# A 4-byte constant that takes 64 bytes, and a last tile finished by halves of columns, in a fused hybrid decoder layer

## The chip, the cores and the metric

The kernel runs on one core of a Trainium2 chip. The metric is the device time of one execution in microseconds; the median of three runs stands for a kernel. One further execution is taken by the hardware profiler, and all rows shown below come from it.

## The reference

The kernel computes one layer of a decoder trunk in float32, for one sequence of 512 positions and a width of 1024. Cut to what matters here:

```python
h = rmsnorm(x, norm_mix_g)
proj = h @ w_in                                  # 1024 x 9232
bg, cg, xv, q, k, v, z, a, b, ga, gb = split(proj)
y_a = (bg * causal_dwconv(cg * xv, conv_a_w)) @ w_a_out
y_b = gated_delta_net(q, k, v, z, a, b) @ w_b_out     # 8 heads, chunked scan
x = x + (sigmoid(ga) * y_a + sigmoid(gb) * y_b) @ w_o
h = rmsnorm(x, norm_ffn_g)
up = causal_dwconv(h @ w_up, ffn_conv_w)         # 1024 x 5632
gate, val = split(up)
x = x + (silu(gate) * val) @ w_down              # 2816 x 1024
out = rmsnorm(x, norm_final_g)
```

## The kernel before, in words

**Products.** Each float32 factor is split into a rounded part and a rest, both of type float32r (`wh` and `wl` for weights, pairs such as `hT0/hT1`, `xs0/xs1` for activations). A product is three TensorE matmuls: rest by rounded, rounded by rest, rounded by rounded. All of them go through one helper, `mm`, so in the profile they share line L108 and are told apart by their tiles' names. In the name "ps<-hT,wh" the two operands stand in the order of the alphabet. A matmul has a stationary operand of 128 by 128, loaded by a weight load of its own (PEld), and a moving operand of 512 or 256 columns.

**Stages, in order.** The input products with `hT` (q, k, v, z, gates; the delta-net scan runs between them), the sum jobs on `ts` and `hT` (Winograd-like forms with moving tiles of 256 columns, `sum_job`), the product with `w_a_out` on `yas`, with `w_b_out` on `yb`, with `w_o` on `mix` and `mixb`, the products with `w_up` on `h` (tiles `h20`, `h21`) and sum jobs on `us`, and last the product with `w_down` on `xs`. In the products with `hT`, `h`, `ts`, `us`, `yas` and `yb` the weights are stationary and the activations move; in those with `mix`, `mixb` and `xs` the activations are stationary and the weights move, 512 columns at a time.

**Where tiles lie.** Tiles come from pools that are stacked from the low end of each partition's memory, or from the high end where a pool says `side="right"`. Each buffer is rounded up to 32 bytes. The pool `const` lies lowest; its first tile is `gate`, 4 bytes on one partition, which takes 32 bytes (1152 to 1184). After it come `ident`, `nhalf`, `phalf`, `wA` and `wF`, and then the pool `wp` with `raw`, `wh` and `wl`, from byte 2816, which is 0 modulo 64. All large tiles of the low stack (`raw`, `wh`, `wl`, `hT`, `yb`, `h2`, `x1`, `kqs` and the delta-net's tiles) start at 0 modulo 64; the tiles of x in the first stage stand at 32. The high stack ends at byte 229344, which is 32 modulo 64, and its large tiles (`ts`, `us`, `xs`, `yas`, `ya`, `mixa`, `mix`, `mixb`, `aTa`, `aTb`) all start at 32 modulo 64. Slices that a matmul takes of a tile start at multiples of 512 bytes within it.

**The order of work.** DMAs, ScalarE (ACT), VectorE (DVE) and GpSimd (POOL) instructions are placed by a list scheduler that follows the order of the program and data dependences; within `tc.manual_schedule` the named engines keep the written order. `gate` is written by `feed`, a one-element GpSimd copy that makes the GpSimd queue wait for a weight block before it issues further DMAs.

**The end.** The product with `w_down` runs in jobs: `use_a` (first pass), `use_c`, `use_b` for all pairs of rows but the last `LAST` = 4, then `use_t(0)`, `use_t(1)` and `use_l` for these four. There are four tiles of 128 positions, t = 0 to 3, with 1024 columns in two halves of 512 (`HALVES`). `use_t(1)` finishes the accumulation of tiles 0 and 1 and calls `fin2` for each; `use_l` finishes the lower half of tiles 2 and 3, which stand in the PSUM banks `v4[0]` and `v4[1]`, 12 matmuls of 512 columns each, and calls `fin2`. The upper halves of tiles 2 and 3 stand in the banks `r[0]` and `r[1]`; they were finished after `use_c` by `fin2_hi`, which leaves the partial norm in `st["r", t]` and the half, multiplied by the norm's weights but not yet by r, in `st["y", t][1]`, so those banks are free by then. For each half, `fin2` adds the bank to `x1`, squares and sums it on ACT, multiplies by the norm's weights on DVE, then forms r (DVE), raises it to -0.5 (POOL), scales one half on DVE and one on ACT, and issues two output DMAs from the SP queue.

Of the kernel before, what the change touches and what calls it, by code (L numbers as in the profile page):

```python
# [9 lines left out]
F32 = mybir.dt.float32  # L10
F32R = mybir.dt.float32r
AF = mybir.ActivationFunctionType
ALU = mybir.AluOpType
# [3 lines left out]
P = 128  # L17
S = 512
NT = S // P
D = 1024  # L20
# [5 lines left out]
EPS = 1e-6  # L26
# [34 lines left out]
def layer_kernel(ctx, tc, x, norm_mix_g, w_in, w_ab, conv_a_w, gdn_conv_w, gdn_A_log, gdn_dt_bias,  # L61
                 gdn_norm_g, w_a_out, w_b_out, w_o, norm_ffn_g, w_up, ffn_conv_w, w_down,
                 norm_final_g, out):
    nc = tc.nc
    pe, act, dve, pool = nc.tensor, nc.scalar, nc.vector, nc.gpsimd
    x2 = x[0]
    out2 = out[0]
# [3 lines left out]
    const = ctx.enter_context(tc.tile_pool(name="const", bufs=1))  # L71
# [4 lines left out]
    def nm(s):  # L76
        cnt[0] += 1
        return f"{s}{cnt[0]}"
# [8 lines left out]
    def advance(queue, n):  # L87
        while n and queue:
            queue[0].step()
            if queue[0].done:  # L90
                queue.popleft()
            else:
                n -= 1

    def tick():
        advance(backs, 1)
        advance(mids, 1)
        advance(chains, 1)
        advance(evacs, 2)
        advance(splits, 1)  # L100
        advance(sums_of, 1)
# [5 lines left out]
    def mm(o, a, b, start, stop, free=False):  # L107
        pe.matmul(o, lhsT=a, rhs=b, start=start, stop=stop, skip_group_check=free)  # L108
        nmm[0] += o.shape[-1]
        if nmm[0] >= SLAB * S:  # L110
            nmm[0] -= SLAB * S
            tick()
# [12 lines left out]
    class Block:  # L125
# [78 lines left out]
    def run_jobs(jobs):  # L204
        jobs[1][0].load()
        for i, (block, use) in enumerate(jobs):
            Task(block.split()).finish()
            drain(splits)
            if i + 1 < len(jobs):
                splits.append(Task(jobs[i + 1][0].split()))  # L210
            for j, (later, _) in enumerate(jobs[i + 2:i + 5]):
                if later.lead >= j + 2:
                    later.load()
            if adds and i + 2 < len(jobs) and jobs[i + 2][0].fed:
                feed(jobs[i + 2][0].raw)
            use(block.wh, block.wl)


    gate = const.tile([1, 1], F32, name="gate")

    def feed(raw):
        el = raw[0:1, 1].rearrange("p k n -> p (k n)") if len(raw.shape) == 4 else raw[0:1, 1]
        tc.keep_in_program_order(pool.tensor_copy(out=gate, in_=el[:, 0:1]))  # L223
        advance(adds, FEED)


# [43 lines left out]
    def sum_job(w, i, xs, sums, consume, place, pre=None):  # L270
        def use(wh, wl):
# [73 lines left out]
    nhalf = const.tile([P, 8], F32, name="nhalf")  # L345
# [11 lines left out]
    def pair_out():  # L357
        return room["pool"].tile([P, 2 * S], F32, tag="o", bufs=room.get("o", 3), name=nm("o"))
# [22 lines left out]
    HS = S // 2  # L381
# [633 lines left out]
    st = {}  # L1015
# [7 lines left out]
    LAST = 4  # L1023
# [176 lines left out]
    FORMS_A, FORMS_T, FORMS_B = (("v2", 1), ("v3", 2), ("v1", 3)), (("21", 0), ("22", 2)), (("v4", 1),)  # L1200
# [41 lines left out]

    def times_b(banks, xs, slot, names, tau, wh, wl, q=None, start=False, stop=False):
        for name, i in names:
            o, w = banks["11" if name == "21" else name][tau], name if q is None else (name, q)
            times(o, xs, slot, i, tau, wh[w], wl[w], start and name != "21", stop, name == "21")

    def open_banks(banks, names):
        for name in names:
# [47 lines left out]
    HALVES = [slice(0, S), slice(S, D)]  # L1297
# [167 lines left out]
    def prep_d(prep, c):  # L1465
        return Task(prep(ffn_pairs(down_w.pairs[2 * c], 2), xs(), 2 * c % 4))
# [28 lines left out]
    def use_b(p):  # L1495
        def use(wh, wl):
            if p % 2 == 0 and p // 2 + 1 < N7 // 2:
                splits.append(prep_d(prep_b, p // 2 + 1))
            for name in (*FORMS_T, *FORMS_B):
                for tau in range(2):  # L1500
                    times_b(d_banks, xs(), p % 4, (name,), tau, wh, wl)
            if p == N7 - LAST - 1:
                splits.append(prep_d(prep_b, N7 // 2 - 1))
        return use


    def use_t(q):
        def use(wh, wl):
            for tau in range(2):
                for i in range(2):  # L1510
                    times_b(d_banks, xs(), (N7 - LAST + 2 * q + i) % 4, FORMS_T, tau, wh, wl, i, False, q + i == 2)
                if q == 1:
                    fin2(tau, [d_banks["11"][tau], d_banks["22"][tau]])
        return use

    def use_l(wh, wl):
        for tau in range(2):
            for i in range(LAST):
                times_b(d_banks, xs(), (N7 - LAST + i) % 4, FORMS_B, tau, wh, wl, i, False, i == LAST - 1)
            fin2(tau + 2, [d_banks["v4"][tau]])  # L1520

    def fin2_hi(t):
        cvp, x1, a = st["cvp"], st["x1"], d_banks["r"][t - 2]
# [10 lines left out]
        yield  # L1534

    def fin2(t, acc):
        cvp, x1 = st["cvp"], st["x1"]
        ss = cvp.tile([P, 2], F32, tag="ss", name=nm("ss"))
        if t < 2:
            o = pair_out()  # L1540
            y, r = [o[:, sl] for sl in HALVES], cvp.tile([P, 1], F32, tag="r", name=nm("r"))
        else:
            y, r = st["y", t], st["r", t]
        for hf, a in enumerate(acc):
            sl = HALVES[hf]
            dve.tensor_tensor(out=x1[:, t, sl], in0=x1[:, t, sl], in1=a, op=ALU.add)
            act.activation(out=a, in_=x1[:, t, sl], func=AF.Square, accum_out=ss[:, hf:hf + 1])
            dve.tensor_tensor(out=y[hf], in0=x1[:, t, sl], in1=st["gfn"][:, sl], op=ALU.mult)
            if hf < len(acc) - 1:
                dve.tensor_scalar(r, ss[:, hf:hf + 1], 1.0 / D, EPS, op0=ALU.mult, op1=ALU.add)  # L1550
        dve.scalar_tensor_tensor(out=r, in0=ss[:, len(acc) - 1:len(acc)], scalar=1.0 / D, in1=r,
                                 op0=ALU.mult, op1=ALU.add)
        pool.tensor_tensor(out=r, in0=r, in1=nhalf[:, 0:1], op=ALU.pow)
        dve.tensor_scalar(y[0], y[0], r, None, op0=ALU.mult)
        act.activation(out=y[1], in_=y[1], func=AF.Copy, scale=r)
        for sl, e in zip(HALVES, y):
            nc.sync.dma_start(out=out2[t * P:(t + 1) * P, sl], in_=e)


    def down_place(i):  # L1560
# [69 lines left out]
```

## Time and profile before

| | before |
|---|---|
| median of three runs | 972.78 us (971.88 to 973.0) |
| the profiled execution's own time | 973.09 us |
| its span, first to last instruction | 971.4 us |
| granted TensorE clock, mean | 0.996 |
| PE busy | 958.7 us (99%) |
| PEld busy | 826.1 us (85%) |
| DVE, ACT, POOL busy | 744.0, 506.7, 153.4 us |
| DMA moved | 138.11 MB, mean 142 GB/s |

PE is the matmul part of TensorE, PEld its weight loads. Matmuls are pipelined: the duration of one (the third number of a group, in ns) is longer than the distance from its start to the next one's start, so the pace of a stretch is read from first and last start and the count, not from the durations. "Busy" of a group counts overlapped time once only.

### The profile page before, as it was taken

The page shows a single profiled execution, that of the slowest core. Times are in us where ns is not written, and L with a number is a line of the kernel's source. Part 1 is how long each engine was busy: PE and PEld are TensorE (multiplying, and loading weights), DVE is VectorE, ACT ScalarE, POOL GpSimd, SP SyncE. Part 2 cuts the span into 40 slices and gives each one's busy share as a digit, 9 for nine tenths or more (in the row PEclk, how much of TensorE's full clock was granted, in tenths as well). Part 3 has the DMA queues.
Part 4 walks back from the last instruction along what each step waited for, and adds up shares of the span by engine and source line. Part 5 has one row for each costly group of instructions (what it writes and reads, how often), then busy time and mean ns, then how long its engine had stood idle before and what let it go on. Part 6 is the DMA issues. An engine that isn't in the chain of part 4 may idle for free.

```text
span 971.4 us, 16140 instructions
## 1 busy us (share of the span) xinstructions
PE 958.7 (99%) x6166; PEld 826.1 (85%) x6166; DVE 744.0 (77%) x1397; ACT 506.7 (52%) x1071; POOL 153.4 (16%) x251
## 2 busy tenths in 40 slices
PE   8999999999999999999999999999999999999996
PEld 6888887887878889999988888998889998888885
DVE  5968686896725968799853479999978888968775
ACT  6796656565444434344642245555545456546463
POOL 3330300202000212312232100231222210000000
PEclk9999999999999999999999999999999999999999
DMA  6443312213121546756877435594775674075332
GB/s 225 154 138 98 116 53 88 74 58 91 52 88 49 147 121 152 184 151 158 266 222 158 119 120 207 165 244 155 164 185 177 180 154 137 37 282 204 99 130 87
DMA packets 51629, 138.11 MB, mean 142 GB/s; under 512 B 21691, under 2 KB 22112, under 8 KB 42848
## 3 DMA queue, kind: packets, MB, share of 16 engines
q1 hardware_dynamic: 39008, 107.72, 32.3%
q0 software_dynamic: 12544, 29.37, 16.1%
q8 instruction: 48, 0.79, 0.3%
q14 instruction: 29, 0.24, 0.1%
HBM read 133.64 MB, written 32.78 MB: 171 GB/s over the span
## 4 chain that ended last, share of the span: by engine, by line
PE 91%; DVE 3%; ACT 1%; issue 1%; POOL 1%; POOLq 0%
PE ps L108 83%; PE ps L681 1%; PE ps L716 1%; DVE wl L141 1%; PE ps L890 1%; PE ps L910 1%; DVE h L1326 0%; PE ps L899 0%; DVE hn L1312 0%; PE ps L878 0%; PE ps L877 0%; PE ps L854 0%; PE ps L848 0%; POOL r L1310 0%; PE ps L792 0%
## 5 line engine op out<-in xcount | busy, mean ns | idle before, releaser
L108 PE MATMUL ps<-hT,wh 128*128 128x512 f32 (+1 forms) x1104 | 319.3, 369 | 1.6 <-ACT hT L499 1.4
L140 ACT CAST wh<-raw 128x512 fp32r<-128x512 f32 x350 | 203.5, 618 | 212.6 <-PE ps L108 149.1
L141 DVE TENSOR_TENSOR wl<-raw,wh 128x512 fp32r<-128x512 f32 x350 | 233.0, 690 | 58.9 <-ACT wh L140 57.7
L108 PEld LDWEIGHTS ps<-hT,wh 128*128 128x128 f32 x1104 | 197.5, 190 | 30.6 <-ACT hT L499 1.6
L108 PE MATMUL ps<-hT,wl 128*128 128x512 f32 (+1 forms) x552 | 195.5, 362 | 0.0
L108 PE MATMUL ps<-h,wh 128*128 128x512 f32 (+1 forms) x704 | 177.8, 341 | 0.2 <-DVE h L1326 0.2
L108 PEld LDWEIGHTS ps<-h,wh 128*128 128x128 f32 x704 | 122.3, 189 | 15.4 <-DVE h L1326 0.4
L108 PEld LDWEIGHTS ps<-hT,wl 128*128 128x128 f32 x552 | 104.7, 190 | 13.8
L108 PE MATMUL ps<-h,wl 128*128 128x512 f32 (+1 forms) x352 | 114.6, 341 | 0.0
L108 PE MATMUL ps<-wh,xs 128*128 128x512 f32 x312 | 98.2, 395 | 0.0
L108 PEld LDWEIGHTS ps<-h,wl 128*128 128x128 f32 x352 | 66.6, 189 | 7.6
L108 PEld LDWEIGHTS ps<-wh,xs 128*128 128x128 f32 x312 | 58.5, 187 | 14.3
L108 PE MATMUL ps<-wl,xs 128*128 128x512 f32 x156 | 61.6, 395 | 0.0
L223 POOL COPY gate<-raw 1x1 f32<-1x1 f32 x38 | 16.9, 446 | 279.9 <-DMA raw<-in_w_in_dram 119.3
L108 PE MATMUL ps<-ts,wh 128*128 128x256 f32 x320 | 58.5, 281 | 0.0
L338 DVE SCALAR_TENSOR_TENSOR cv<-ps,wA,cv 128x511 f32<-128x511 f32 (+2 forms) x72 | 53.2, 742 | 4.0 <-ACT cv L335 3.8
L140 ACT CAST wh<-raws 128x512 fp32r<-128x512 f32 x66 | 39.2, 619 | 28.2 <-PE ps L108 16.6
L141 DVE TENSOR_TENSOR wl<-raws,wh 128x512 fp32r<-128x512 f32 x66 | 43.1, 689 | 13.4 <-ACT wh L140 13.3
L161 DVE TENSOR_TENSOR raw<-raw 128x512 f32<-128x512 f32 x72 | 49.5, 688 | 1.4
L108 PEld LDWEIGHTS ps<-ts,wh 128*128 128x128 f32 x320 | 49.8, 188 | 0.0
L108 PE MATMUL ps<-us,wh 128*128 128x256 f32 x256 | 46.8, 281 | 0.0
L108 PE MATMUL ps<-yas,wh 128*128 128x512 f32 x128 | 40.4, 395 | 0.0
(310 smaller groups left out, 1548.5 us busy)
## 6 DMA issues: line engine op xcount, KB each, us to landing
raw<-in_w_in_dram SPq DMA_DIRECT2D x35, 1024.0 KB, 4.8
raw<-in_w_up_dram SPq DMA_DIRECT2D x22, 1024.0 KB, 5.7
dv<-in_w_down_dram POOLq DMA_DIRECT2D x50, 256.0 KB, 6.0
raws<-dv SPq DMA_DIRECT2D x8, 768.0 KB, 6.8
ov<-in_w_o_dram POOLq DMA_DIRECT2D x20, 256.0 KB, 5.3
raws<-in_w_down_dram SPq DMA_DIRECT2D x10, 512.0 KB, 4.1
raw<-in_w_a_out_dram SPq DMA_DIRECT2D x4, 1024.0 KB, 5.2
raw<-in_w_b_out_dram SPq DMA_DIRECT2D x4, 1024.0 KB, 5.7
```

The lines of the kernel that those rows point to most:

```text
L108: pe.matmul(o, lhsT=a, rhs=b, start=start, stop=stop, skip_group_check=free)
L140: act.copy(out=wh, in_=src)
L141: dve.tensor_tensor(out=wl, in0=src, in1=wh.bitcast(F32), op=ALU.subtract)
L161: dve.tensor_tensor(out=r[q], in0=a, in1=b, op=op)
L223: tc.keep_in_program_order(pool.tensor_copy(out=gate, in_=el[:, 0:1]))
L338: dve.scalar_tensor_tensor(out=dst[:, sh:], in0=src[:, :S - sh], scalar=wcol(j), in1=dst[:, sh:], op0=ALU.mult, op1=ALU.add)
L681: pe.transpose(out=o[:, n * P:(n + 1) * P], in_=src[:, n * P:(n + 1) * P], identity=ident)
L716: pe.matmul(o[:, i], lhsT=kqs[:, a, h, 0, sl], rhs=kqs[:, b, h, :, sl], start=a > 0, stop=a + b == 0)
L890: pe.matmul(o[:, 0:P], lhsT=TTf[:, f, :], rhs=rs[h], start=True, stop=True)
L910: pe.matmul(o[:, 0:P], lhsT=A[:, f, :], rhs=vns[h], start=True, stop=True)
```

## The change

The tile `gate` is declared with 16 elements instead of one, so it takes 64 bytes instead of 32, and all that lies above it in the low stack moves up by 32 bytes. The high stack stays. Only one element of `gate` is written, as before.

The end is rewritten. `use_b` marks the accumulation of `v4` as stopped after its last pair. At the start of `use_t(1)` one DVE instruction adds the right 256 columns of `v4[1]` to `x1`. `use_l` finishes tile 2 as before, with 12 matmuls of 512 columns; tile 3 then runs in two parts of 256 columns, 12 matmuls each: the left one accumulates on in `v4[1]`, the right one starts afresh in the bank `r[0]`. Each part has its own add, square and step of r; the order of DVE, ACT, POOL and SP is written out by hand; half 0 of tile 2 is scaled on ACT and half 1 on DVE, half 0 of tile 3 on DVE and half 1 on ACT; the last output DMA is issued from the ACT queue. `fin2` keeps only tiles 0 and 1, with the same instructions.

```diff
-    gate = const.tile([1, 1], F32, name="gate")
+    gate = const.tile([1, 16], F32, name="gate")
...
-        tc.keep_in_program_order(pool.tensor_copy(out=gate, in_=el[:, 0:1]))
+        tc.keep_in_program_order(pool.tensor_copy(out=gate[:, 0:1], in_=el[:, 0:1]))
...
-    def times(o, xs, slot, i, tau, wh, wl, start=False, stop=False, free=False):
+    def times(o, xs, slot, i, tau, wh, wl, start=False, stop=False, free=False, cols=slice(0, S)):
         xh, xl = (e[:, slot, i, tau * P:(tau + 1) * P] for e in xs)
         for k, (a, b) in enumerate(((xl, wh), (xh, wl), (xh, wh))):
-            mm(o, a, b, start and k == 0, stop and k == 2, free)
+            mm(o[:, cols], a, b[:, cols], start and k == 0, stop and k == 2, free)
...
+    LO, HI = slice(0, HS), slice(HS, S)
+
     def use_t(q):
         def use(wh, wl):
+            if q == 1:
+                x1 = st["x1"]
+                dve.tensor_tensor(out=x1[:, 3, HI], in0=x1[:, 3, HI], in1=d_banks["v4"][1][:, HI], op=ALU.add)
...
     def use_l(wh, wl):
-        for tau in range(2):
+        x1, gfn = st["x1"], st["gfn"]
+
+        def mult(t, cols):
+            dve.tensor_tensor(out=st["y", t][0][:, cols], in0=x1[:, t, cols], in1=gfn[:, cols], op=ALU.mult)
+
+        def scale(t, hf, on_act, queue):
+            y, r = st["y", t][hf], st["r", t]
+            if on_act:
+                act.activation(out=y, in_=y, func=AF.Copy, scale=r)
+            else:
+                dve.tensor_scalar(y, y, r, None, op0=ALU.mult)
+            queue.dma_start(out=out2[t * P:(t + 1) * P, HALVES[hf]], in_=y)
+
+        def power(t):
+            pool.tensor_tensor(out=st["r", t], in0=st["r", t], in1=nhalf[:, 0:1], op=ALU.pow)
+
+        def part(t, e, a, cols, between):
+            r = st["r", t]
+            ss = st["cvp"].tile([P, 2], F32, tag="ss", name=nm("ss"))
             for i in range(LAST):
-                times_b(d_banks, xs(), (N7 - LAST + i) % 4, FORMS_B, tau, wh, wl, i, False, i == LAST - 1)
-            fin2(tau + 2, [d_banks["v4"][tau]])
+                times_b(d_banks, xs(), (N7 - LAST + i) % 4, FORMS_B, t - 2, wh, wl, i, e == 1 and i == 0, i == LAST - 1,
+                        cols, a)
+            dve.tensor_tensor(out=x1[:, t, cols], in0=x1[:, t, cols], in1=a[:, cols], op=ALU.add)
+            act.activation(out=a[:, cols], in_=x1[:, t, cols], func=AF.Square, accum_out=ss[:, e:e + 1])
+            between()
+            dve.scalar_tensor_tensor(out=r, in0=ss[:, e:e + 1], scalar=1.0 / D, in1=r, op0=ALU.mult, op1=ALU.add)
+
+        def between():
+            mult(3, LO)
+            scale(2, 0, True, nc.sync)
+
+        with tc.manual_schedule(engines={mybir.EngineType.DVE, mybir.EngineType.Activation, mybir.EngineType.Pool,
+                                         mybir.EngineType.SP}):
+            part(2, 0, d_banks["v4"][0], slice(0, S), lambda: mult(2, slice(0, S)))
+            power(2)
+            part(3, 0, d_banks["v4"][1], LO, between)
+            part(3, 1, d_banks["r"][0], HI, lambda: mult(3, HI))
+            power(3)
+            scale(2, 1, False, nc.sync)
+            scale(3, 0, False, nc.sync)
+            scale(3, 1, True, nc.scalar)
```

More of the change, by code (lines that the diff above doesn't have):

```diff
@@ L1241, in times_a, with times_b @@
                 times(banks[name][tau], xs, slot, i, tau, wh[name], wl[name], start, stop)
-    def times_b(banks, xs, slot, names, tau, wh, wl, q=None, start=False, stop=False):
+    def times_b(banks, xs, slot, names, tau, wh, wl, q=None, start=False, stop=False, cols=None, to=None):
         for name, i in names:
             o, w = banks["11" if name == "21" else name][tau], name if q is None else (name, q)
-            times(o, xs, slot, i, tau, wh[w], wl[w], start and name != "21", stop, name == "21")
+            times(o if to is None else to, xs, slot, i, tau, wh[w], wl[w], start and name != "21", stop, name == "21" or bool(cols),
+                  cols or slice(0, S))
     def open_banks(banks, names):
@@ L1500, in use @@
                 for tau in range(2):
-                    times_b(d_banks, xs(), p % 4, (name,), tau, wh, wl)
+                    times_b(d_banks, xs(), p % 4, (name,), tau, wh, wl, None, False,
+                            p == N7 - LAST - 1 and name in FORMS_B)
             if p == N7 - LAST - 1:
@@ L1536, in fin2 @@
     def fin2(t, acc):
-        cvp, x1 = st["cvp"], st["x1"]
+        cvp, x1, y = st["cvp"], st["x1"], pair_out()
         ss = cvp.tile([P, 2], F32, tag="ss", name=nm("ss"))
[L1539 to L1552, printed above, removed]
+        r = cvp.tile([P, 1], F32, tag="r", name=nm("r"))
+        for hf, sl in enumerate(HALVES):
+            dve.tensor_tensor(out=x1[:, t, sl], in0=x1[:, t, sl], in1=acc[hf], op=ALU.add)
+            act.activation(out=acc[hf], in_=x1[:, t, sl], func=AF.Square, accum_out=ss[:, hf:hf + 1])
+            dve.tensor_tensor(out=y[:, sl], in0=x1[:, t, sl], in1=st["gfn"][:, sl], op=ALU.mult)
+            if hf == 0:
+                dve.tensor_scalar(r, ss[:, 0:1], 1.0 / D, EPS, op0=ALU.mult, op1=ALU.add)
+        dve.scalar_tensor_tensor(out=r, in0=ss[:, 1:2], scalar=1.0 / D, in1=r, op0=ALU.mult, op1=ALU.add)
         pool.tensor_tensor(out=r, in0=r, in1=nhalf[:, 0:1], op=ALU.pow)
[L1554 to L1557, printed above, removed]
+        dve.tensor_scalar(y[:, HALVES[0]], y[:, HALVES[0]], r, None, op0=ALU.mult)
+        act.activation(out=y[:, HALVES[1]], in_=y[:, HALVES[1]], func=AF.Copy, scale=r)
+        for sl in HALVES:
+            nc.sync.dma_start(out=out2[t * P:(t + 1) * P, sl], in_=y[:, sl])
     def down_place(i):
```

## The prediction

> **What bounds the kernel now.** I read the profile's page first, then the chain that ended last, then the rows of single tiles.
>
> ```profile
> span 971.4 us, 16140 instructions
> PE 958.7 (99%) x6166; PEld 826.1 (85%) x6166; DVE 744.0 (77%) x1397; ACT 506.7 (52%) x1071; POOL 153.4 (16%) x251
> ...
> PE 91%; DVE 3%; ACT 1%; issue 1%; POOL 1%; POOLq 0%
> ```
>
> TensorE is busy all the time and is 91% of the chain. So the pace at which one matmul follows the next is what the time is made of. The chain in order of time shows where that holds without a break:
>
> ```profile
> 316.16 282.05 PE ps L108 x1635
> 598.24 1.41 DVE o L1260 x2
> ...
> 631.29 1.23 DVE xf L251
> ...
> 633.18 324.38 PE ps L108 x1777
> ```
>
> From 316 to 598 us and from 633 us to the end the chain is nothing but matmuls. From 598.24 to 633.18 it runs through DVE (the evacuations after the first half of `w_o`, the norm, the turns), and PE only works beside it. A faster matmul there is worth nothing.
>
> Now the pace. Two stages have the same number of matmuls, the same shape, and weights from the same buffers; only the moving tile differs. First the rows of the tile `yas`, then those of `yb` (duration min/median/max in ns, then first and last start):
>
> ```profile
> L108 PE MATMUL ps<-yas,wh x128: 395/395/397, 489.4 to 534.0; 128*128 128x512 f32 x128
> L108 PE MATMUL ps<-yas,wl x64: 396/396/397, 489.6 to 532.1; 128*128 128x512 f32 x64
> L331 ACT CAST yas<-ya x8: 608/615/622, 476.4 to 481.3; 128x512 fp32r<-128x512 f32 x8
> L332 DVE TENSOR_TENSOR yas<-ya,yas x8: 680/684/686, 478.0 to 483.1; 128x512 fp32r<-128x512 f32 x8
> ```
>
> ```profile
> L108 PE MATMUL ps<-yb,wh x128: 389/389/396, 534.2 to 577.5; 128*128 128x512 f32 x128
> L108 PE MATMUL ps<-yb,wl x64: 389/389/397, 534.4 to 575.7; 128*128 128x512 f32 x64
> ...
> L331 ACT CAST yb<-yb x8: 607/620/622, 490.1 to 493.8; 128x512 fp32r<-128x512 f32 x8
> L332 DVE TENSOR_TENSOR yb<-yb,yb x8: 682/684/693, 490.8 to 495.0; 128x512 fp32r<-128x512 f32 x8
> ```
>
> 192 matmuls make 191 steps: with `yas` 44.6 us, or 233.5 ns a step; with `yb` 43.3 us, or 226.7 ns. `yas` starts at 32 modulo 64 and the weights at 0; `yb` and the weights both start at 0. In the last stage the parts are exchanged: `xs`, at 32, is stationary and the weights, at 0, move.
>
> ```profile
> L108 PE MATMUL ps<-wh,xs x312: 388/394/397, 854.5 to 963.4; 128*128 128x512 f32 x156
> ```
>
> With the half as many of `wl` these are 468 matmuls, 467 steps in 108.9 us: 233.2 ns, the same as with `yas`. That the price is one whichever operand stands at 32 speaks for the relation of the two, not for the place of one.
>
> For moving tiles of 256 columns the sign is the other. Two adjacent windows of a sum job, first matmuls with `ts` (at 32), then with `hT` (at 0), weights at 0 in both; the columns are length, PE busy, count, clock, DMA share, GB/s:
>
> ```profile
> 379.14:384.82 5.68, 5.68 (x48) 1.00 0.96 149
> ...
> 384.82:389.12 4.30, 4.30 (x36) 1.00 0.72 242
> ```
>
> Unlike: 5.68/48 = 118.3 ns. Alike: 4.30/36 = 119.4 ns.
>
> The counts, by form (each `wh` group has half as many with `wl` beside it, since a product is three matmuls, two with `wh`):
>
> ```profile
> L108 PE MATMUL ps<-hT,wh 128*128 128x512 f32 x800 | 260.5, 400 | 0.0
> ...
> L108 PE MATMUL ps<-h,wh 128*128 128x512 f32 x384 | 119.8, 389 | 0.0
> ...
> L108 PE MATMUL ps<-h,wh 128*128 128x256 f32 x320 | 60.8, 284 | 0.2 <-DVE h L1326 0.2
> L108 PE MATMUL ps<-hT,wh 128*128 128x256 f32 x304 | 60.0, 287 | 1.6 <-ACT hT L499 1.4 <-DVE hT L503 0.3
> L108 PE MATMUL ps<-ts,wh 128*128 128x256 f32 x320 | 58.5, 281 | 0.0
> L108 PE MATMUL ps<-us,wh 128*128 128x256 f32 x256 | 46.8, 281 | 0.0
> ...
> L108 PE MATMUL ps<-wh,mix 128*128 128x512 f32 x88 | 28.2, 396 | 0.0
> ...
> L108 PE MATMUL ps<-wh,mixb 128*128 128x512 f32 x24 | 8.3, 398 | 0.0
> ```
>
> **The change, part one: 32 bytes.** It adds no instruction. Everything in the low stack goes from 0 to 32 modulo 64 and the high stack stays at 32, so every pair of weights and activations becomes alike, but at 32, and no pair of large matmul operands at 32 and 32 is in this trace. Its price is bounded by 226.7 (as two at 0) and 233.5 (as one at 32). I take 226.7, since exchanging the operands left the price at 233.2 and 233.5, which a price for the place of each operand would make a coincidence.
>
> Unlike matmuls of 512 columns: `xs` 468, `yas` 192, `mix` 132, `mixb` 36, together 828. 12 of them (tile 3) are split and counted below. From the end of `yb` at 577.7 to 598.24, 88 of the `mix` ones fit at 233 ns; the other 80 of `mix` and `mixb` lie beside the DVE chain and are counted at nothing (0.5 us more if that chain moves with them). That leaves 736. At 6.5 ns each (a little under 233.2 or 233.5 less 226.7): −4.78 us. Unlike ones of 256 columns: `ts` 480 and `us` 384, 864 at +1.1 ns: +0.95 us, all in the two unbroken stretches. Pairs that were alike (`hT`, `h`, `yb`) stay alike: nothing.
>
> ACT and DVE work on shifted tiles too. The rows L331 and L332 above are the same work on tiles at 32 (`yas`) and at 0 (`yb`): 615 against 620 and 684 against 684 ns. So nothing there, and if a few ns came, both run beside PE (DVE 77% busy). DMAs into `raw` are hidden by blocks loaded two to four jobs ahead; the page shows PE without a wait for one.
>
> **Part two: the end.** The rows of the timeline:
>
> ```profile
> 962.27 0.73 ACT L1555 ACTIVATE o<-o,r 128x512 f32<-128x512 f32 x1 [0.85 <-POOL r L1553]
> ...
> 962.90 0.58 ACT L1547 ACTIVATE ps<-x 128x512 f32<-128x512 f32 x1
> ...
> 963.45 0.39 PE L108 MATMUL ps<-wh,xs 128*128 128x512 f32 x1
> 963.64 0.16 DVE L1551 SCALAR_TENSOR_TENSOR r<-ss,r 128x1 f32<-128x1 f32 x1 [0.28 <-ACT ps L1547]
> ...
> 964.45 0.49 DVE L1554 TENSOR_SCALAR y<-y,r 128x512 f32<-128x512 f32 x1 [0.65 <-POOL r L1553]
> 964.85 0.68 DVE L1546 TENSOR_TENSOR x<-x,ps 128x512 f32<-128x512 f32 x1
> ...
> 965.62 0.60 ACT L1547 ACTIVATE ps<-x 128x512 f32<-128x512 f32 x1 [0.46 <-DVE x L1546]
> 966.16 0.19 ACT L1547 ACTIVATION_READ_ACCUMULATOR ps<-x 128x1 f32 x1
> 966.38 0.16 DVE L1551 SCALAR_TENSOR_TENSOR r<-ss,r 128x1 f32<-128x1 f32 x1
> 966.62 0.54 POOL L1553 TENSOR_TENSOR r<-r,nhalf 128x1 f32<-128x1 f32 x1 [2.21 <-DVE r L1551]
> 967.20 0.72 ACT L1555 ACTIVATE y<-y,r 128x512 f32<-128x512 f32 x1 [0.85 <-POOL r L1553]
> ```
>
> ```profile
> 967.72 0.81 SPq L1557 DMA_DIRECT2D out_dram<-y  x2
> ```
>
> The last matmul ends at 963.84, but tile 3's add starts at 964.85: DVE stood at 964.45 with tile 2's scaling, waiting for POOL. Then add, square, r, power, scale and DMA follow in a row. PE itself: 12 matmuls of 233.2 become 24 of 119.4, +0.07 us. The new add of a quarter tile in `use_t(1)` falls where DVE waits for PE and costs nothing; without that cover, 0.42 us (the 256-column row below).
>
> ```profile
> L293 DVE TENSOR_TENSOR u<-ps,u 128x256 f32<-128x256 f32 x18 | 7.6, 422 | 1.4 <-ACT u L292 1.1
> ...
> L292 ACT COPY u<-ps 128x256 f32<-128x256 f32 x18 | 6.7, 372 | 28.3 <-PE ps L108 28.3
> ```
>
> The written order puts tile 2's step of r (963.64, held by ACT, which scales tile 1 at 962.27 before it squares tile 2 at 962.90) ahead of tile 3's adds. From 963.80 on: left add 0.42, to 964.22; left square about 0.38 (estimate, from the copy's 0.37) and its read; its step of r to 964.96; right add from 964.96 to 965.38, 1.1 us after the last matmul; ACT meanwhile scales tile 2 from 964.8 to 965.5 and squares the right part to 965.9; step of r 966.07 to 966.23, power to about 966.85, scales from 966.88 (before: 967.20). ACT ends at 967.6 and issues the last DMA itself, where the second of SP's two began about 968.13. So the end comes 0.3 to 0.5 us sooner; I take −0.5. The best end is bounded by the matmuls (adds not held: −1.5), the worst by one more instruction of 0.5 us on DVE and a dearer issue from ACT, which no row shows (+0.5).
>
> **Sum.** −4.78 + 0.95 + 0.07 − 0.5 = −4.26 us. The profiled execution took 973.09 us by its own account (span 971.4), so 968.8; the median of the runs stands 0.31 below it: 968.5 us.
>
> The Trainium skill, in "TensorE: Matmul & The Clock Gate", section "Part 2: What happens when you issue a matmul", holds that the moving operand and the weights come in through two independent read ports and that loading the next weights takes nothing from the running matmul. By that rule how the two stand to each other could not matter, and part one would bring nothing, which gives 972.35 us, the same as the first rival. The trace does not agree in so far as `yas` and `yb` differ by 6.8 ns a step, but it can't exclude that the cause is another one.
>
> **Rivals.**
> 1. The pace doesn't come from the place modulo 64. All slow tiles lie in the high stack, so the cause could be which end of the memory they lie in. Then only the end changes: 973.09 + 0.07 − 0.5 − 0.31 = 972.35. For it: place and end are confounded in this trace. Against it: the operands at 32 slow 512 columns and speed 256, as a phase between two streams would, rather than a slow region. The Trainium skill's rule of two ports (the page named above) leads to the same time.
> 2. The slower one: an operand at 32 costs by itself, and two at 32 are no better than one. Then the 828 gain nothing, and the alike ones lose: `hT` 1200, `h` 576, `yb` 192, together 1968 at 6.5 ns, +12.8 us; their 936 of 256 columns gain 1.1 ns each, −1.0; with the end, 973.09 + 12.8 − 1.0 − 0.43 − 0.31 = 984.1. It decides from 229 ns on: at 2.2 ns above 226.7 the 1968 eat up the whole 4.26 us. For it: no pair at 32 has been seen. Against it: the price didn't change with the operand that stood at 32.
> 3. The pace comes as forecast, but the scheduler places tile 1's scaling ahead of the hand-written part, so that all of the end waits: +0.5 instead of −0.5, 969.5.
>
> **Chances.** Forecast 0.70, rival 3 0.05, rival 1 0.12, rival 2 0.13. The likeliest case's own range is 966.8 to 969.8: 0.5 us for the DVE stretch, up to 1 us each way for the end, 0.9 if the 256-column loss stays out. To leave out no more than 2 in 10 the range must take in rival 1: 966.8 to 972.7. A measurement of this kernel can't tell less than about 0.2% (1.95 us) from no change; forecast and rival 3 are faster by more, 0.75; rival 1 is within, 0.12; rival 2 is slower, 0.13.
>
> **What would show it.** The rows of `yas`, `xs` and `mix` at 226 to 228 ns a step and 389 ns duration; `yb`, `h`, `hT` unchanged; windows of `ts` at 119.4. `yb` at 231 or more is rival 2; `yas` at 233 is rival 1. At the end, tile 3's second add within 1.2 us of the last matmul and the last scale about 3.0 us after it (before: 3.36). The forecast is wrong first if two operands at 32 don't pace like two at 0.

## The result and the profile after

| | before | after |
|---|---|---|
| median (six runs each, same chip) | 971.87 us (970.99 to 973.0) | 965.13 us (964.45 to 967.54) |
| ratio after / before | | 0.9934, 95% interval 0.9921 to 0.9947 |
| the profiled execution's own time | 973.09 us | 966.41 us |
| its span | 971.4 us | 964.7 us |

The change makes the kernel 6.7 us faster. The forecast was 968.5 us, and its range began at 966.8: the direction came true, the size did not. Some 0.9 us of the gap between 968.5 and 965.13 are not the change's: the forecast started from 972.78 for the kernel before, which these six runs put at 971.87. One kernel below, with ten buffers for the weights, took 1920.87 and 2443.0 us in two of its six executions, at a granted clock of 1.00 in both; its 969.06 us is the median of the other four, and its paces are read from the same kernel run once more.

The page of after, its span and busy times, then the shares of its chain:

```profile
span 964.7 us, 16169 instructions
...
PE 951.5 (99%) x6178; PEld 822.6 (85%) x6178; DVE 743.1 (77%) x1401; ACT 505.9 (52%) x1073; POOL 157.1 (16%) x251
...
PE 91%; DVE 4%; ACT 1%; issue 1%; POOL 1%; POOLq 0%
```

PE does 12 matmuls more (the split of the last tile) and is busy for 7.2 us less: the matmuls follow each other faster. The chain in order of time shows where this can count:

```profile
315.98 279.38 PE ps L108 x1635
595.39 1.39 DVE o L1261 x2
...
628.55 1.23 DVE xf L251
630.43 317.85 PE ps L108 x1765
948.30 1.38 DVE x L1586 x2
```

The form is that of before: two stretches of nothing but matmuls, and the DVE stretch between them. The first matmul stretch begins where it did (315.98, before 316.16), so all but 0.2 us of the gain lies behind this point. From 948.3 us on, 9 us ahead of the last matmul's end, the chain runs through DVE, ACT and POOL.

Which stage gave it? The rows of `yas`, `yb` and `xs` (duration min/median/max in ns, first and last start in us) are three answers:

```profile
L108 PE MATMUL ps<-yas,wh x128: 394/394/394, 486.9 to 531.5; 128*128 128x512 f32 x128
```

```profile
L108 PE MATMUL ps<-yb,wh x128: 388/389/393, 531.7 to 575.0; 128*128 128x512 f32 x128
```

```profile
L108 PE MATMUL ps<-wh,xs x320: 276/388/392, 849.9 to 957.0; 128*128 128x512 f32 x152, 128*128 128x256 f32 x8
L108 PE MATMUL ps<-wl,xs x160: 279/394/394, 850.1 to 956.9; 128*128 128x512 f32 x152, 128*128 128x256 f32 x8
```

`yas` takes 44.6 us for its 191 steps, as before: 233.5 ns from these rounded starts (233.3 from the unrounded ones, in both kernels), although it and the weights now both stand at 32 modulo 64. `yb` is unchanged (43.3 us, 226.7 ns). From the starts of all its matmuls of 512 columns, `xs` goes at 228.9 ns, neither the old 233.2 nor 226.7. And the windows of a sum job, the same stretches as shown of before, of `ts` alone and of `hT` alone (columns: length, PE busy, count, clock, DMA share, GB/s):

```profile
378.73:384.19 5.46, 5.46 (x48) 1.00 0.83 135
```

```profile
384.19:388.49 4.30, 4.30 (x36) 1.00 0.74 244
```

`hT` stays at 4.30/36 = 119.4 ns. `ts` went from 118.3 to 5.46/48 = 113.7 ns, against a forecast of 119.4. The granted clock is 1.00 in all four windows, and `hT` and `yb` keep their paces in the same trace, so the clock has no part in it.

Stage by stage, from the first matmul of one stage to that of the next, in the two profiled executions:

| stage | before | after | difference | the forecast's term |
|---|---|---|---|---|
| up to the first `ts` | 358.25 | 358.07 | -0.2 | 0 |
| sum jobs on `ts` and `hT` | 131.13 | 128.86 | -2.3 | +0.5 |
| `yas` | 44.81 | 44.80 | 0.0 | -1.25 |
| `yb` | 43.55 | 43.54 | 0.0 | 0 |
| `mix`, `mixb`, DVE stretch | 40.94 | 40.42 | -0.5 | -0.6 |
| `h` and sum jobs on `us` | 235.80 | 234.22 | -1.6 | +0.4 |
| `xs`, to the last matmul's end | 109.36 | 107.35 | -2.0 | -2.9 |
| from there to the last instruction | 7.54 | 7.44 | -0.1 | -0.5 |

The differences sum to -6.7 us, the terms to -4.3. (The terms split the forecast's 736 into 456 for `xs`, 192 for `yas` and 88 for `mix`, at 6.5 ns each.)

The end, from the timeline of after:

```profile
957.22 0.42 DVE L1547 TENSOR_TENSOR x<-x,ps 128x256 f32<-128x256 f32 x1
...
958.14 0.71 ACT L1533 ACTIVATE y<-y,r 128x512 f32<-128x512 f32 x1
...
958.35 0.41 DVE L1547 TENSOR_TENSOR x<-x,ps 128x256 f32<-128x256 f32 x1
...
958.85 0.39 ACT L1548 ACTIVATE ps<-x 128x256 f32<-128x256 f32 x1
...
959.63 0.72 POOL L1539 TENSOR_TENSOR r<-r,nhalf 128x1 f32<-128x1 f32 x1 [1.71 <-DVE r L1550]
960.39 0.72 ACT L1533 ACTIVATE y<-y,r 128x512 f32<-128x512 f32 x1 [1.02 <-POOL r L1539]
960.39 0.48 DVE L1535 TENSOR_SCALAR y<-y,r 128x512 f32<-128x512 f32 x1 [0.43 <-POOL r L1539]
961.14 0.37 ACTq L1536 DMA_DIRECT2D out_dram<-y  x1
```

The last matmul ends at 957.26. The second add of tile 3 starts 1.09 us later, the last two scales 3.13 us later (before: 3.36), and ACT issues the last DMA 3.88 us after it (the second of SP's two, before: 4.30). Then 0.25 us are given back: the last packet of that DMA arrives 2.11 us after its issue, where the last one from SP took 1.86 in the kernel before.

### The profile page after: what moved, and what is told of

The parts are those of the page before. It is cut to its first block, busy times and chain, and to the rows that moved or that the text cites. A ratio compares the mean times of both kernels' runs of the same rounds, so it can differ in the third digit from the quotient of the medians.

```text
span 964.7 us, 16169 instructions
## 1 busy us (share of the span) xinstructions
PE 951.5 (99%) x6178; PEld 822.6 (85%) x6178; DVE 743.1 (77%) x1401; ACT 505.9 (52%) x1073; POOL 157.1 (16%) x251
## 4 chain that ended last, share of the span: by engine, by line
PE 91%; DVE 4%; ACT 1%; issue 1%; POOL 1%; POOLq 0%
PE ps L108 83%; PE ps L681 1%; PE ps L716 1%; DVE wl L141 1%; PE ps L890 1%; PE ps L910 1%; DVE h L1327 1%; PE ps L899 0%; DVE hn L1313 0%; PE ps L878 0%; PE ps L877 0%; PE ps L854 0%; PE ps L848 0%; POOL r L1311 0%; PE ps L792 0%
## 5 line engine op out<-in xcount | busy, mean ns | idle before, releaser
L108 PE MATMUL ps<-wh,xs 128*128 128x512 f32 (+1 forms) x320 | 96.9, 384 | 0.0
L223 POOL COPY gate<-raw 1x1 f32<-1x1 f32 x38 | 19.7, 518 | 272.9 <-DMA raw<-in_w_in_dram 119.7
L108 PE MATMUL ps<-wl,xs 128*128 128x512 f32 (+1 forms) x160 | 62.1, 388 | 0.0
L108 PE MATMUL ps<-ts,wh 128*128 128x256 f32 x320 | 56.2, 276 | 0.0
```

The lines of the kernel that those rows point to most:

```text
L223: tc.keep_in_program_order(pool.tensor_copy(out=gate[:, 0:1], in_=el[:, 0:1]))
```

## The experiments

In all of them **distance** means the start of the moving operand less the start of the stationary one, in bytes within a partition, modulo 256. It comes from the addresses in the compiled program. Before: weights at 19200, `ts` and `yas` at 135136; 135136 - 19200 = 115936 = 452 x 256 + 224, so the distance is 224. In the stages where weights move over `mix` and `xs` it is 32, its complement. After: weights at 19232, distance 192, and 64 for `mix` and `xs`. For `hT`, `h` and `yb` it is 0 in both. Slices start at multiples of 512, so one number holds for a whole stage. A pace is the mean from one matmul's start to the next one's, over all pairs of neighbours of a stage in the trace; for `mix` it is taken up to the DVE stretch.

A time below that has no ratio beside it is of a single run, and it carries a reading only beside its paces.

**The parts by themselves.** First the change of `gate` alone, in the kernel before:

```diff
-    gate = const.tile([1, 1], F32, name="gate")
+    gate = const.tile([1, 16], F32, name="gate")
```

> Only the constant takes 64 bytes; the end is as before. Both theories (pace set by the distance of the two operands, or by the place of each) expect the pace of the changed kernel: `ts` and `us` 113.7 ns a step, `xs` and `mix` 228.9, `yas` 233.3, so 6.5 to 6.9 us less than before. The rival that the new end brought part of it expects under 6 us.

Measured: 966.28 us, ratio 0.9936 (0.992 to 0.9953). Next the new end alone, with `gate` at its old 4 bytes:

```diff
-    gate = const.tile([1, 16], F32, name="gate")
+    gate = const.tile([1, 1], F32, name="gate")
```

> Only the new end; the constant takes 32 bytes as before. Read from the two traces, the end (from the last matmul's end to the last instruction) takes 7.45 us against 7.54, and 24 matmuls of 256 columns take the place of 12: expected within 0.3 us of before. If the new end is worth the 0.5 us forecast, 0.5 us less.

Measured: 971.59 us, ratio 0.9994 (0.9985 to 1.0003). So the 32 bytes bring all that can be told from no change. From the last matmul to the last instruction, e1 with the old end takes 7.76 us and the kernel before 7.54; with the new end it is 7.44 (after), 7.29 (this one), and 7.29 to 7.45 in the other kernels below. Some 0.1 to 0.5 us are the end's share.

**Not the place, not "alike modulo 64".** The whole kernel is moved down by 32 bytes: all big tiles stand at 0 modulo 64 again, with the distances of the changed kernel.

```diff
-    gate = const.tile([1, 16], F32, name="gate")
+    gate = const.tile([1, 1], F32, name="gate")
...
+                st["sc"].tile([P, 8], F32, tag="pad", bufs=1, name="padsc")
...
+        up.tile([P, 8], F32, tag="pad", bufs=1, name="padup")
```

> The changed kernel with the constant back at 32 bytes and the two high pools lowered by 32 bytes: every operand at 0 modulo 64, but the same distances as in the changed kernel (115904 from weights to `yas` and `ts`). Theory of distance: the same pace as the changed kernel, `ts` 113.7, `xs` 228.9, `yas` 233.3. Theory of place (32 is good, 0 is bad, or the other way): another pace, for `ts` 118 to 120.

Measured: 965.17 us; 113.74 ns for `ts` and `us`, 233.33 for `yas`, 228.89 for `xs`, each within 0.02 ns of the changed kernel's. Its row of `yas`:

```profile
L108 PE MATMUL ps<-yas,wh x128: 394/394/395, 485.9 to 530.4; 128*128 128x512 f32 x128
```

Both operands stand at 0 modulo 64, and it goes at 233 ns. Then the opposite: everything at 32 modulo 64 as in the changed kernel, but the high stack 192 bytes lower, so that all distances are 0 (pads of 48 elements in the same two places, `gate` as changed).

> The changed kernel with the high pools lowered by 192 bytes: still at 32 modulo 64, but the distance from weights to `ts`, `yas`, `us`, `xs`, `mix` becomes a multiple of 512, as it is between weights and `hT`, `h`, `yb`. Theory of distance: `yas`, `xs`, `mix` at 226.7 ns a step and `ts`, `us` at 119.4, so about 2 us less than the changed kernel on the first and 4.9 more on the second, 967 to 969 us. Theory of place or of the high end of the memory: the pace of the changed kernel, unchanged.

Measured: 967.32 us. Rows of `yas` and of the window of one `ts` stretch:

```profile
L108 PE MATMUL ps<-yas,wh x128: 389/389/390, 487.9 to 531.2; 128*128 128x512 f32 x128
```

```profile
376.80:382.56 5.76, 5.76 (x48) 1.00 0.81 123
```

`yas` and `xs` go at 226.7 ns, as `yb` does, and `ts` and `us` lose all they had gained: 5.76/48 = 120.0 ns. The residue modulo 64 is the same 32 here as in the changed kernel, so it sets nothing. The high stack is as high as ever, so its end of the memory sets nothing either. What changed is the distance.

**The other distances.** Three kernels differ from the changed one in the pads alone: 16 and 32 elements (distance 128 for `ts`, `yas` and `mix`, 64 for `us`, 192 for `xs`), 64 and 8 (192, but 448 modulo 512, for `ts` and `yas`; 160 for `us`, 96 for `xs`), 40 and 24 (32 for `ts` and `yas`, 224 for `mix`, 96 for `us`, 160 for `xs`).

> The changed kernel with the pool of `ts`, `yas`, `mix` lowered by 64 bytes and that of `us`, `xs` by 128: moving less stationary address is 128 modulo 512 for `ts` and `yas`, 384 for `mix`, 64 for `us`, 448 for `xs`. Theory that only the distance modulo 128 counts: `ts`, `yas`, `mix` as at 0 (120.0, 226.7, 226.7), `us` 113.7 as at 192, `xs` between the values seen at 192 and 320 (228.9 to 233.3). Theory that it counts modulo 256 or 512: `ts`, `yas` and `mix` differ from the values at 0, and `us` (64) from 113.7.

> The changed kernel with the pool of `ts`, `yas`, `mix` lowered by 256 bytes and that of `us`, `xs` by 32: 448 modulo 512 for `ts` and `yas`, 64 for `mix`, 160 for `us`, 352 for `xs`. Theory that the distance counts modulo 256 (or 128): `ts` 113.7, `yas` 233.3 and `mix` 228.9, all as in the changed kernel (192 and 320). Theory that it counts modulo 512: other values.

> The changed kernel with the pool of `ts`, `yas`, `mix` lowered by 160 bytes and that of `us`, `xs` by 96: 32 modulo 512 for `ts` and `yas`, 480 for `mix`, 96 for `us`, 416 for `xs`. No theory forecasts the values between; if odd multiples of 32 are always bad for 512 columns, `yas`, `mix` and `xs` run at 231 to 234, and if modulo 256 is right, `mix` (480, so 224) runs at 233.3 as `yas` did before the change.

Measured: 971.32, 970.11 and 974.07 us; the last is above the 972.13 of the kernel before beside it, but within the 970.82 to 975.79 of that kernel's eleven runs, so it is not shown to be slower. With before, after and the distance 0 they give this table (ns from start to start):

| distance modulo 256 | 512 columns | 256 columns |
|---|---|---|
| 0 | 226.7 | 119.4 to 120.0 |
| 32 | 233.3 | 117.9 |
| 64 | 228.9 | 117.9 |
| 96 | 233.3 | 119.9 |
| 128 | 232.4 to 233.3 | 118.7 |
| 160 | 234.3 | 117.4 |
| 192 | 233.3 | 113.7 (117.8 below) |
| 224 | 233.3 | 118.3 |

At 512 columns 0 is best and 64 next; all others cost some 7 ns. At 256 columns 192 is best, and 0 and 96 are the worst. Nothing in the order of the distances says this beforehand. That the modulus is no larger than 256 is seen from the second of the three: `ts` at 448 modulo 512 goes at 113.74 ns and `yas` at 233.34, as at 192. Stages of different roles agree: 32 is `yas` in one kernel (233.35) and `xs` in the kernel before, with the weights moving (233.33). At 256 columns that does not hold throughout. The column of the table is `ts`, `us`, `hT` and `h`; the 24 matmuls of tile 3 at the end, where the weights move over `xs` and run behind 512 columns, go at 116.7 ns at distance 32, 118.7 at 160 and 117.8 at 192.

**Each at its best.** `ts` and `us` at 192, `yas`, `mix` and `xs` at 0: the two tiles of each pair go into one, 192 bytes longer, and `ts` and `us` start 192 bytes into it.

```diff
-            st["ts"] = [sc.tile([P, 4, 4, HS], F32R, tag=f"t{i}", name=f"ts{i}") for i in range(2)]
+            st["ts"] = halves_of(sc.tile([P, 8240], F32R, tag="tt", name="tsp"), 48, 4)
...
-            st["yas"] = [st["sc"].tile([P, ND, S], F32R, tag=f"t{i}", name=f"yas{i}") for i in range(2)]
+            st["yas"] = halves_of(st["sc"].tile([P, 8240], F32R, tag="tt", name="yasp"), 0, ND, False)
```

> The changed kernel with two distances: the pairs `ts0/ts1`, `yas0/yas1`, `mix0/mix1` share one buffer of 32960 bytes, and so do `us0/us1`, `xs0/xs1`; in it `ts` and `us` stand 192 bytes further up than `yas`, `mix` and `xs`, so 192 modulo 512 for the moving tiles of 256 columns and 0 for the pairs of 512. Theory of distance: `ts`, `us` 113.7 and `yas`, `mix`, `xs` 226.7 to 226.8; against the changed kernel 192 at 6.6 ns, 132 at 2.2 and 456 at 2.2 less, 2.5 us: 962 to 963 us, 9 us less than before. Theory of place: no difference from the changed kernel.

Measured: 963.92 us (962.71 to 964.49), ratio 0.9912 (0.9898 to 0.9927): faster than before, and by its median 1.2 us faster than the changed kernel, where 2.5 were expected; the two intervals overlap. In the traces, from the first `ts` matmul to the last matmul's end, it takes 596.6 us against 599.2, so the 2.5 are there. The paces are 113.74 ns for `ts` and `us` and 226.67 for `yas` and `xs`. The row of its `yas`:

```profile
L108 PE MATMUL ps<-yasp,wh x128: 389/389/389, 485.8 to 529.1; 128*128 128x512 f32 x128
```

With its last DMA issued from SP instead of ACT (`scale(3, 1, True, nc.sync)`):

> The kernel with both distances, its last output DMA issued from SP instead of ACT. If the ACT queue makes the landing slower, the last DMA lands 2.2 us after its issue (2.48 from ACT) and is issued 0.05 to 0.4 us later; the tail from the last matmul to the last instruction is then 7.2 to 7.6 us (7.44). If the 2.48 us have nothing to do with the queue, landing stays at 2.4 to 2.5 and the tail is 7.5 to 7.8.

Measured: 963.52 us, one run. The issue comes 4.06 us after the last matmul (3.88 from ACT), the last packet 1.92 us after it (2.11): 5.98 and 5.99 us, the same sum. The tail is 7.38 us against 7.44. The queue is a wash.

**A forecast from the table that failed.** In the sum jobs `hT` and `h` still go at 120 ns, with moving tiles that other products share. Here the weights' buffers are 256 bytes longer, and the sum jobs' weights stand 64 bytes into them, which gives `hT` and `h` the distance 192 there. Room comes from giving up one buffer of twelve each for `wh` and `wl`, two of four each for `r` and `vn`, and one temporary; pads of 48 elements keep all pairs of 512 columns at 0.

```diff
-WQ = 12
+WQ = 11
...
-            wh = self.wh[name] = wp.tile([P, *self.quarter], F32R, tag="wh", bufs=WQ, name=nm("wh"))
+            wh = self.wh[name] = self.buffer("wh")
...
+            t = wp.tile([P, 576], F32R, tag=tag, bufs=WQ, name=nm(tag))[:, self.shift:self.shift + 512]
...
+            self.shift = 16
```

> The weights' buffers are 2304 bytes long, and in the sum jobs the weights stand 64 bytes into them. Moving less stationary address modulo 256: 192 for the 648 hT/h matmuls of 256 columns in the sum jobs and for the 864 of ts/us, 0 for every pair of 512 columns (hT, h, yb, yas, mix, mixb, xs). 11 buffers for weights instead of 12, fewer for r, vn and one temporary. Theory (the distance modulo 256 sets the pace, for each pair by itself): hT/h of the sum jobs go from 119.9 and 120.3 to 113.7 ns, ts/us stay at 113.7, 512 columns stay at 226.7; against the kernel with both distances (963.9 us) that is 648 x 6.3 = 4.1 us less, 959.8 us, if a buffer less makes PE wait for nothing. Rival (the pace of 256 columns hangs on the tile ts/us or on its stage, not on the distance): hT/h stay at 120, 963.9 us. If the missing buffer is felt, PE shows waits for raw or wh that were not there, and the control shows the same.

Beside it the control, `self.shift = 0`:

> The same buffers as in the kernel with all pairs at their best, but the weights at their start in the sum jobs too: every distance is 0 modulo 256. Theory: 256 columns at 120 ns in all stages and 512 at 226.7, as in the kernel with distance 0 (967.3 us); what it is above that is the price of the fewer buffers. The kernel with all at their best should be 1512 matmuls x 6.2 = 9.4 us faster than this one.

Measured: 968.54 us (ratio 0.9953, 0.9939 to 0.9967), and 974.74 for the control, against 959.8 expected of the first. Two things went another way. One is the buffers. In the control the first `ts` matmul starts at 363.5 us, in the kernels with the old buffers at 355.8 to 358.4; 3.2 us of that is a wait of PE that the kernels with twelve buffers don't have (columns: us in total, times, longest; this row is of the kernel with the shift, and the control has the same):

```profile
PE ps L108 <- DVE kn L710: 3.2, 1, 3.2
```

The other is the pace. Windows of one `ts` stretch and of the `hT` stretch behind it:

```profile
381.41:387.06 5.65, 5.65 (x48) 1.00 0.89 134
```

```profile
387.06:391.30 4.24, 4.24 (x36) 1.00 0.74 237
```

Both stand at 192 and go at 117.8 ns: `hT` gained 1.6 to 2 ns instead of 6, and `ts` lost 4. Three causes were open: the place of the pair (stationary at 96, moving at 32 modulo 256), the buffers' stride of 2304 bytes, and something that differs between neighbouring stretches. First the same kernel, all moved by 160 bytes (`gate` of 56 elements, pads of 8):

> As the kernel with all pairs at their best, all buffers moved by the same amount: the moving tiles of 256 columns at 192 modulo 256, their weights at 0 (distance 192 as there, stride 2304 as there); all 512-column pairs at 192 and 192. Theory (place counts for 256 columns): 113.7 ns for ts, us and the sum jobs' hT and h instead of 117.8, 1512 x 4.05 = 6.1 us less than that kernel's 968.5: 962.4. Rival (the stride of 2304 counts): 117.8 again, 968.5. The paces of 512 columns stay at 226.7 by both.

Measured: 969.86 us (ratio 0.9979, 0.997 to 0.9989), 117.78 ns again. Its operands stand where those of the kernel moved down by 32 bytes do (weights at 0, `ts` at 192 modulo 256), which ran at 113.74, so the place by itself does not set this. Then the kernel with each at its best, moved to the suspected place, with buffers of the old length (`gate` of 32, pads of 48, three buffers for `r`):

> The kernel with both distances (ts/us at 192, all else at 0), all moved by 64 bytes: weights at 96, ts/us at 32 modulo 256, buffers of 2048 bytes, three buffers for r instead of four. Theory (place): ts/us at 117.8 ns instead of 113.7, 864 x 4.05 = 3.5 us more than 963.9: 967.4; 512 columns at 226.7. Rival (stride): ts/us stay at 113.7, 963.9.

Measured: 963.7 us; the window of a `ts` stretch:

```profile
378.62:384.08 5.46, 5.46 (x48) 1.00 0.93 141
```

5.46/48 = 113.7 ns at the suspected place: the place is out a second time. Ten buffers instead of eleven, with `r`, `vn` and the temporary as they were:

> As the kernel with all best at 192, but ten buffers for weights instead of eleven, and the buffers for r, vn and the temporary as in the changed kernel. If the wait of 3.2 us for kn comes from r and vn, it is gone, and the time is 3 us or more below the one with eleven (about 959.5 if 256 columns go at 113.7); if it comes from the weights' buffers, it is as long or longer, and the time the same or above.

Measured: 969.06 us (ratio 0.9964, 0.995 to 0.9977), so nothing is won back. Since `wh` and `wl` of a block lie an odd multiple of 256 bytes apart in the kernels with eleven long buffers, the next suspicion was a jump between 192 and 448 modulo 512 from matmul to matmul. 256 unused bytes between the two groups of buffers take it away; with ten buffers it isn't there:

> As the kernel with all best at 192, with 256 unused bytes between the buffers of wh and those of wl, so that both parts of a block of weights stand alike modulo 512. Theory (the jump by 256 from one matmul to the next keeps the pace at 117.8): ts, us and the sum jobs' hT and h at 113.7 to 115.5 ns (a block still jumps against the next one, and in the changed kernel a stretch takes some four steps from 120 down to 113.7), the span 3.5 to 6 us below that kernel's 966.9. Rival (the length of the buffers or something else that goes with it): 117.8 as before, the span the same.

> The kernel with ten weight buffers, all best at 192, once more: wh and wl of a block are alike modulo 512 here too (ten buffers of 2304 bytes between them). Theory (jump): 113.7 to 115.5 ns for the matmuls of 256 columns at distance 192; with the 967.5 to 969.7 us measured, waits of PE of 3 us or more that the kernels with eleven do not show. Rival: 117.8 ns.

Measured: 971.52 and 971.47 us, 117.8 ns in both. The jump is out too. With ten buffers (the second of the two, the kernel of the 969.06 us once more) the wait for `kn` is 3.5 us, so it does not come from `r` and `vn`; that it comes from the weights' buffers is likely, but was not tried by itself.

The stretches read step by step show what is left. In the changed kernel every `ts` stretch begins behind `hT` of 256 columns at distance 0, and its steps are 121, 121, 116, 114, 114, 113, 113, 114 ns. In the kernels with the shift the sum job begins behind matmuls of 512 columns at 0, with `hT` at 192, and goes at 117 to 119 ns from the first step on to the last. So one distance has two steady paces, and what ran before would choose between them. A kernel above, with buffers of the old length, agrees: in the one with distance 128 for `ts`, the matmuls of tile 3 stand at 192, run behind 512 columns at 192, and go at 117.8 ns from the first steps on; but there the weights move. The test: long buffers without the shift, and the distances of the kernel with each at its best, so that `ts` at 192 again follows `hT` at 0.

> Buffers of 2304 bytes, all weights at their start; distances as in the kernel with both distances: ts/us at 192, all else at 0 (mixb at 64), so that ts and us follow hT and h of 256 columns at 0. Theory (what runs before sets the pace at 192): ts/us go 121, 121, 116, 114 and on at 113.7 ns, the span 864 x 6.3 = 5.4 us below that of the control with these buffers (973.0): 967.6. Rival (the stride of the buffers): ts/us at 117.8 from the first steps, 1.9 us below it: 971.1.

Measured: 967.51 us, span 965.8; the 967.6 expected was for the span. From the first `ts` matmul to the last matmul's end it takes 596.3 us, the control 602.1: 5.8 us less, where 5.4 were expected. The window of a `ts` stretch:

```profile
382.73:388.19 5.46, 5.46 (x48) 1.00 0.87 129
```

113.7 ns, with first steps of 120, 122, 116, 114: the stride by itself is out, and the history of the stretch is what fits. At distance 192 a run of 256-column matmuls settled at 113.7 ns where it was entered from 120 ns at distance 0, and at 117.8 where it was entered with the sum job's `hT` at 192 too, from 512 columns. One thing stays open: together with `hT`'s distance this kernel also takes back the 64 bytes by which the weights stood inside the longer buffers, and the two were not changed one at a time.

## Why the prediction was right and wrong, point by point

**What bounds the kernel: right.** TensorE's pace outside the DVE stretch was nearly the whole matter: 5.9 of the 6.7 us are the `ts`, `us` and `xs` stages, all in the unbroken stretches. One reading was not exact: "to the end" the chain is not all matmuls. Its row of before ends at 957.56 us (633.18 + 324.38), 6.3 us ahead of the last matmul's end.

**The price of two operands at 32: the step that failed.** "... every pair of weights and activations becomes alike, but at 32 ... I take 226.7". The residue modulo 64 was the wrong variable. In the trace of before "alike" always meant distance 0 and "unlike" always 224 or 32, two distances that happen to cost the same. I took this equality for a sign that only "alike or not" counts, and chose between the bounds 226.7 and 233.5 with it. The change set no distance to 0; it moved 224 to 192 and 32 to 64. `yas` so stayed at 233.3 (-1.25 forecast, 0.0 measured), and `xs` got 4.4 ns a step instead of 6.5 (-2.9 forecast, -2.0 measured).

**256 columns: wrong in sign.** +1.1 ns a step was forecast for `ts` and `us`, -4.6 measured: 864 x 5.7 = 4.9 us of difference. This term alone takes the time out of the range, which allowed for the loss to stay out (0.9 us) but for no gain: 118.3 and 119.4 were the only two prices in the trace, and I took the change to be a move from the one to the other. It was a move to a distance that the trace did not hold, and its price lay outside both. That the kernel became faster, as forecast, is thus in part luck: the largest share of the gain, 3.9 us on `ts` and `us`, came where a loss had been forecast.

**What stays alike: right.** `yb` went 43.55 to 43.54 us, `hT` stayed at 119.4 ns, and the rows of ACT and DVE that work on `yb`, which moved (L331, L332), took 628 and 687 ns (620 and 684 before), with nothing of it to be seen in the stage behind them.

**The DVE stretch: right in the count, by luck near in size.** 88 of the `mix` steps were counted, -0.6; -0.5 came. But `mix` went from 233.3 to 228.9 ns, 4.4 a step and not 6.5: up to the start of the DVE stretch 0.4 us are won, and the rest of the 0.5 lies in that stretch, which was counted at nothing.

**The end: right in order, too large in size.** The adds, scales and issues come within 0.2 us of the times worked out, taken from the last matmul. Of the -0.5, -0.1 is left in the profiled pair: the power on POOL took 0.72 us where the 0.54 of before had been assumed, and the last DMA from ACT took 0.25 us longer from its issue to its last packet, the "dearer issue from ACT, which no row shows".

**The rivals.** The first named `yas` at 233 as its sign, and that came, but neither its time (972.35) nor its cause: with the high stack at the same end of the memory, moving it by 192 bytes took `yas` to 226.7. The second needed `yb` at 231; it stayed at 226.7. The third is refuted by the timeline: ACT scales tile 1 ahead of tile 2's square, but so the forecast had it, and what follows comes at the times worked out.

**The rule of two read ports.** The Trainium skill, in "TensorE: Matmul & The Clock Gate", section "Part 2: What happens when you issue a matmul", has the moving operand and the next weights come in independently. The prediction could not exclude another cause for the 6.8 ns. Now it can: with instructions and order alike, pads that move the high stack alone take `yas` from 233.3 to 226.7 ns and `ts` from 113.7 to 120.0. By the rule these would be equal. The runs do not show what inside the chip ties the pace to the distance and to what ran before; that stays open.

## What to carry to other kernels

Where a profile shows two paces for the same instruction, work out for each the addresses of both operands and the distance between them, not the alignment of each. If the planned layout has a distance that the trace does not show, its price may lie outside all the prices seen, in both directions. Give each stage its own distance with a pad, and try the residues in a few kernels, each stage at another one: three kernels were enough here. A layout that suits one number of columns may be the worst for another: distance 0 is the best here for 512 columns and among the worst for 256.

## What the runs showed of the hardware that was not expected

- The pace of float32r matmuls hangs on the distance between moving and stationary operand modulo 256: 226.7 to 234.3 ns at 512 columns, 113.7 to 120.0 at 256, at a granted clock of 1.00 in the windows shown.
- One distance can have two steady paces: 113.7 and 117.8 ns at 192 and 256 columns, most likely by what ran before the stretch. A `ts` stretch of the changed kernel starts at 121 ns and is at 114 from its fourth step on.
- The last packet of a 256 KB output DMA arrived 2.11 us after its issue from ACT's queue, and 1.86 and 1.92 us after its issue from SP's; ACT could issue it 0.2 us sooner, so nothing was won. Each is one execution, and the DMA ahead of it was issued 0.24 us earlier with ACT, 0.42 with SP, so the queue is not shown to be the cause.
